# The modulation's weight transfers issued by GpSimd's queue instead of SyncE's

## The chip, the core and the metric

The kernel runs on one core of a Trainium2 chip. The metric is the time of one execution on the device, in microseconds (us), measured as the median of several runs. The core's engines are PE (TensorE, the matmuls, with its weight loads shown apart as PEld), DVE (VectorE), ACT (ScalarE), POOL (GpSimd) and SP (SyncE). Each engine works through its own row of instructions in order, and a transfer (DMA) is started by an instruction that stands in the row of one of them; what starts transfers is called that engine's queue here. A transfer's time to landing is counted from the start of the instruction that issues it.

## The reference, cut to what is touched

The whole computation is two blocks on 512 tokens of width 1024. The first block is a mixer (an mLSTM and a dilated attention, side by side) followed by a product-key layer of experts (PEER). The second block has two layers, each an attention and a convolutional feed-forward, both modulated by vectors that come from a condition `c`. What the change touches is the making of these vectors:

```
silu_c = jax.nn.silu(c)
silu_cc = jax.nn.silu(c_ctx)
for i in range(DEPTH_2):                      # 2 layers
    mod = silu_c @ w_mod[i] + b_mod[i]        # w_mod[i] is 1024 x 6144, float32
    mod_c = silu_cc @ w_mod[i] + b_mod[i]
    sh1, sc1, gt1, sh2, sc2, gt2 = jnp.split(mod[:, None, :], 6, axis=-1)
    ...
    h = modulate(rmsnorm(x, g_attn[i]), sh1, sc1)
```

Nothing of `mod` depends on `x`, so the kernel makes the vectors of both layers while the first block runs.

## The kernel before

Activations lie transposed, 8 tiles of 128 features by 512 tokens. Most products are made of three matmuls of split operands: a float32 weight tile is loaded (`wload`, lines 186 to 189, tile `wraw`, three buffers), ACT makes its high part `wh` (line 183), DVE the low part `wl` (line 184), and PE runs `hh,wh`, `hl,wh` and `hh,wl` (lines 206 to 208 in `proj`). All transfers of `wload` are issued by SP, in its row's order.

The modulation is the generator `modulation(mp_, pmod, ly)` (line 379 on). For a layer `ly` it goes over 3 groups, 8 steps `k` and 2 halves: 48 transfers of 512 KB each, 96 in all, and each loads a tile `mraw` that is used by four small matmuls (line 392, eight PE rows in the trace: 128x32 weights, 256 columns) and then not again. `mraw` has two buffers, so a transfer is issued as soon as PE has finished the four matmuls of the tile two before it: at any time at most two of these tiles are ahead of PE. At a group's end the sums are copied to `mrow` by ACT (line 397) and transposed by PE (line 347).

`fill(n)` advances the generator by n steps of `k` (two tiles each). It is called between other work: layer 0's 48 tiles are used during the mixer (from the program's start to about 308 us of the trace), layer 1's during the query stage of the experts (about 365 to 555 us). There, for each of 8 heads and each of 2 halves, the kernel issues a transfer of `keys` on POOL (line 854), makes a projection of a `w_query` tile, calls `fill(1 + half)`, runs some early products of experts (line 814), and makes the scores `sc` (line 863), whose best 16 DVE picks (`top16`, lines 841 to 848). After both halves POOL adds candidates (`cand`, line 871), which DVE searches again.

A scheduler of the framework puts the instructions of every engine into order: it gives the work priorities, keeps its own estimate of when each operand is ready, and writes one fixed row per engine. Nothing is reordered on the chip. At the start, POOL's row holds the loads of constants (`cload`, line 161: `ccols`, `cols`, `bmod` and so on), the table of the attention's bias (`t5oh`, `t5ln`, `relb`, lines 445 to 447) and `t5d` (line 453); SP's row holds the eight tiles of `XT`, then `mraw` and the weights. `norm_split` at the start runs with high priority: squares on ACT (line 258), their sum `nsum` on DVE, `ncol` (line 263) and `nbc` (line 271) on PE, then `nh`, `hh` and `hl`, from which the gates' product `gps` (lines 206 to 208) is made.

Of the kernel before, what the change touches and what calls it, by code (L numbers as in the profile page):

```python
# [107 lines left out]
def body(ctx: ExitStack, tc: tile.TileContext, a: dict, out: bass.AP, dbg=None, stop=None):  # L108
# [8 lines left out]
    ve, se, pe, gp, sy = nc.vector, nc.scalar, nc.tensor, nc.gpsimd, nc.sync  # L117
# [41 lines left out]
    def cload(pl, name, shape, dt=F32):  # L159
        t = pl.tile(shape, dt, name=name)  # L160
        gp.dma_start(t, a[name])
        return t
# [183 lines left out]
    def transpose(ps, src):  # L346
        pe.transpose(ps, src, ident[:src.shape[0], :src.shape[0]])  # L347
# [32 lines left out]
    def modulation(mp_, pmod, ly):  # L380

        bm = cload(mp_, "bmod", [128, 2, 48])
        for g in range(3):
            ps = pmod.tile([128, 512], F32, name="mod")
            for k in range(KT):
                for hf in range(2):

                    raw = mp_.tile([128, 4, 256], F32, name="mraw", bufs=2)
                    sy.dma_start(raw, a["w_mod"][ly, g, k, hf])
                    for c in range(4):  # L390
                        o = 32 * c
                        pe.matmul(ps[o:o + 32, hf * 256:hf * 256 + 256], sc[:, k], raw[:, c],  # L392
                                  start=k == 0 and hf == 0, stop=k == KT - 1 and hf == 1, tile_position=(0, o))
                if k < KT - 1:
                    yield
            rows = mp_.tile([128, 512], F32, name="mrow")
            se.activation(rows, ps, AF.Copy)
            tp = pmod.tile([128, 4, 128], F32, name="mod")
            for b_ in range(4):
                transpose(tp[:, b_], rows[:, b_ * 128:(b_ + 1) * 128])  # L400
            tv = tp.rearrange("p b (c r) -> p c b r", c=4)
            s = slice(g * 16, g * 16 + 16)
            bv = bm[:, ly, s].rearrange("p (c b) -> p c b", c=4)
            for dst, r_ in ((modx, 0), (modc, 1)):
                ve.tensor_tensor(dst[:, ly, s].rearrange("p (c b) -> p c b", c=4), tv[:, :, :, r_], bv, OP.add)
            yield
        for m_, gm in ((modx, gmx), (modc, gmc)):
            for i in range(2):
                ve.scalar_tensor_tensor(gm[:, ly, i * 8:i * 8 + 8], m_[:, ly, i * 24 + 8:i * 24 + 16], 1.0,
                                        c2[:, ly, i * 8:i * 8 + 8], OP.add, OP.mult)  # L410
# [13 lines left out]
    with ExitStack() as mx:  # L424
        mp_ = pool(mx, "mod")
        pmod = pool(mx, "pmod", 1, space=PS)
        ho = pool(mx, "mho")
        ml_ = mx.enter_context(ExitStack())
        ph["mod"] = modulation(mp_, pmod, 0)
        hp = pool(ml_, "mh")  # L430
        wk = pool(ml_, "mwork", 2)
# [337 lines left out]
    with ExitStack() as ex:  # L769
# [10 lines left out]
        hf = XT  # L780
# [53 lines left out]
        with ExitStack() as gx:  # L834
            mp_ = pool(gx, "mod")
            kp_ = pool(gx, "topk")
            ph["mod"] = modulation(mp_, pmod, 1)
            v16 = kp_.tile([128, 4, 16, 16], F32, name="v16")
            i16 = kp_.tile([128, 4, 16, 16], U32, name="i16")
# [959 lines left out]
```

## Time and profile before

| | |
|---|---|
| median of 3 runs | 3386.69 us (3386.09 to 3388.05) |
| the profiled execution | 3394.01 us, of which the trace's span is 3391.3 us |
| PE busy | 3279.6 us (97% of the span) |
| DVE busy | 2353.6 us (69%) |
| ACT busy | 1237.5 us (36%) |
| POOL busy | 681.4 us (20%) |

The profiled execution is 7.3 us above the median of the runs, and 2.7 us of it lie around the span. Busy shares are taken over a program with very different stages: the first 36 us, for one, hold the first loads and little for PE to do, and some stages of the mixer and of the experts leave PE idle, while most of the rest is PE end to end. PE's clock is shown as granted, 1.00 for 2.4 GHz and 0.50 for 1.2 GHz.

### The profile page before, as it was taken

To read this page: it belongs to the slowest core of one execution; us is meant where nothing else is said; L and a number is where in the kernel's file an instruction comes from. 1 tells how busy PE (TensorE), PEld (TensorE's weight loads), DVE (VectorE), ACT (ScalarE), POOL (GpSimd) and SP (SyncE) were. 2 spreads that over 40 slices of the span, in tenths; PEclk is the share of its full clock that TensorE was granted. 3 is DMA by queue.
4 is the path that set the end of the run, shared out by engine and by line. 5 is a ranking of instruction groups with operands and counts; after the bars stand their busy time and mean duration, and the time that the engine had idled before them with its cause. 6 is when DMAs were issued, how large, how long until landed. Compare 5 with 4: busy or idle time off the path is not lost.

```text
span 3391.3 us, 49822 instructions
## 1 busy us (share of the span) xinstructions
PE 3279.6 (97%) x19091; PEld 2761.6 (81%) x19091; DVE 2353.6 (69%) x4718; ACT 1237.5 (36%) x2137; POOL 681.4 (20%) x695
## 2 busy tenths in 40 slices
PE   8899999899999999999999999999999998989999
PEld 5565666678999999999989887898888887878887
DVE  6345678876777767777765557677776778758776
ACT  5135211564333333333354546321221246633221
POOL 0000011564444444444411222000000001100000
PEclk9899999999999999999999999999999999999999
DMA  5544564459888889888832222222112110023231
GB/s 172 185 126 158 177 208 149 152 207 330 300 313 309 305 289 331 303 313 315 311 112 76 69 73 66 67 87 63 63 63 66 59 43 28 14 76 118 94 99 56
DMA packets 151990, 538.07 MB, mean 159 GB/s; under 512 B 17988, under 2 KB 23332, under 8 KB 150216
## 3 DMA queue, kind: packets, MB, share of 16 engines
q1 hardware_dynamic: 97920, 326.76, 28.9%
q0 software_dynamic: 52800, 205.51, 17.0%
q8 instruction: 150, 2.46, 0.3%
q10 hardware_dynamic: 1032, 2.62, 0.2%
q14 instruction: 88, 0.72, 0.1%
HBM read 497.24 MB, written 40.13 MB: 158 GB/s over the span
## 4 chain that ended last, share of the span: by engine, by line
PE 86%; DVE 7%; DMA 2%; issue 2%; ACT 2%; POOL 1%; SPq 0%; DVEq 0%; POOLq 0%; ACTq 0%
PE pv L1100 15%; PE acc L206 11%; PE acc L208 11%; PE acc L207 11%; PE acc L232 9%; PE pd L200 3%; PE pd L199 3%; PE pd L201 3%; PE acc L814 3%; PE pt L347 2%; DMA mraw<-in_w_mod_dram 2%; PE mod L392 2%; PE gps L978 1%; PE on L1401 1%; DVE eb L960 1%
## 5 line engine op out<-in xcount | busy, mean ns | idle before, releaser
L206 PE MATMUL acc<-hh,wh 128*128 128x512 f32 (+1 forms) x1728 | 636.4, 369 | 6.3 <-DVE cg L1206 2.3
L207 PE MATMUL acc<-hl,wh 128*128 128x512 f32 (+1 forms) x1728 | 632.4, 366 | 0.0
L208 PE MATMUL acc<-hh,wl 128*128 128x512 f32 (+1 forms) x1728 | 632.1, 366 | 0.0
L206 PEld LDWEIGHTS acc<-hh,wh 128*128 128x128 f32 x1728 | 325.4, 188 | 52.6 <-issue 7.9
L207 PEld LDWEIGHTS acc<-hl,wh 128*128 128x128 f32 x1728 | 325.4, 188 | 38.8 <-issue 0.9
L208 PEld LDWEIGHTS acc<-hh,wl 128*128 128x128 f32 x1728 | 325.0, 188 | 38.6 <-issue 2.2
L183 ACT ACTIVATE wh<-wraw 128x1024 fp32r<-128x1024 f32 (+1 forms) x189 | 199.2, 1055 | 401.2 <-PE acc L207 174.1
L1100 PE MATMUL pv<-vh,al 128*128 128x512 f32 x768 | 301.0, 392 | 0.0
L1100 PE MATMUL pv<-vl,ah 128*128 128x512 f32 x768 | 300.7, 392 | 0.0
L1100 PE MATMUL pv<-vh,ah 128*128 128x512 f32 x768 | 298.8, 389 | 0.0
L184 DVE TENSOR_TENSOR wl<-wraw,wh 128x1024 fp32r<-128x1024 f32 (+1 forms) x189 | 230.8, 1222 | 97.6 <-ACT wh L183 94.0
L1016 POOL DMA_INDIRECT rows<-in_expert_v_dram,sidx x128 | 193.9, 1515 | 231.9 <-DVE tok L1031 198.3
L1016 POOL DMA_INDIRECT rows<-in_expert_u_rows_dram,sidx x128 | 176.8, 1382 | 238.1 <-DVE rows L1021 214.4
L232 PE MATMUL acc<-wh,hh 128*128 128x256 f32 (+1 forms) x624 | 195.9, 315 | 3.9 <-ACT hh L183 2.3
L232 PE MATMUL acc<-wh,hl 128*128 128x256 f32 (+1 forms) x624 | 193.6, 310 | 0.0
L232 PE MATMUL acc<-wl,hh 128*128 128x256 f32 (+1 forms) x624 | 193.3, 310 | 0.0
L1074 DVE TENSOR_TENSOR al<-ge,ah 128x384 fp32r<-128x384 f32 x128 | 71.5, 559 | 163.2 <-ACT ah L1072 162.6
L1072 ACT ACTIVATE ah<-ge 128x384 fp32r<-128x384 f32 x128 | 67.3, 526 | 317.4 <-PE pv L1100 284.4
L1100 PEld LDWEIGHTS pv<-vh,al 128*128 128x128 f32 x768 | 144.1, 188 | 30.2
L1031 DVE SCALAR_TENSOR_TENSOR tok<-rows,spre,tok 128x1024 f32<-128x1024 f32 x127 | 162.6, 1280 | 7.3 <-DMA rows<-in_expert_v_dram,sidx 6.6
L1100 PEld LDWEIGHTS pv<-vl,ah 128*128 128x128 f32 x768 | 144.2, 188 | 28.1
L1100 PEld LDWEIGHTS pv<-vh,ah 128*128 128x128 f32 x768 | 144.4, 188 | 27.7
(459 smaller groups left out, 7355.2 us busy)
## 6 DMA issues: line engine op xcount, KB each, us to landing
wraw<-in_expert_u_dram SPq DMA_DIRECT2D x128, 512.0 KB, 6.2
vraw<-in_expert_v_dram SPq DMA_DIRECT2D x127, 512.0 KB, 4.8
mraw<-in_w_mod_dram SPq DMA_DIRECT2D x96, 512.0 KB, 4.3
wraw<-in_ffn_up_dram SPq DMA_DIRECT2D x88, 512.0 KB, 3.6
gt<-gdr POOLq DMA_DIRECT2D x31, 768.0 KB, 9.4
wraw<-in_ffn_down_dram SPq DMA_DIRECT2D x44, 512.0 KB, 4.1
gdr<-gst POOLq DMA_DIRECT2D x6, 2048.0 KB, 7.4
gdr<-rows POOLq DMA_DIRECT2D x6, 2048.0 KB, 7.7
```

Source lines behind the costliest of these rows:

```text
L183: se.activation(hi, src, AF.Copy)
L184: ve.tensor_tensor(lo, src, hi.bitcast(F32), OP.subtract)
L199: pe.matmul(ps, wh[i], xh[i], start=i == 0, stop=False)
L200: pe.matmul(ps, wh[i], xl[i], start=False, stop=False)
L201: pe.matmul(ps, wl[i], xh[i], start=False, stop=i == n - 1)
L206: pe.matmul(ps, wh[:, k], hh[:, k], start=k == 0, stop=False)
L207: pe.matmul(ps, wh[:, k], hl[:, k], start=False, stop=False)
L208: pe.matmul(ps, wl[:, k], hh[:, k], start=False, stop=k == KT - 1)
L232: pe.matmul(ps[:, i], x[:, k, s], y, start=k == 0 and i == 0 and x is hh and y is wh, stop=k == KT - 1 and i == nt - 1 and y is wl)
L1016: gp.indirect_dma_start(r, None, src, bass.IndirectOffsetOnAxis(ap=sidx[:, k:k + 1], axis=0))
L1031: pin(ve.scalar_tensor_tensor(o, r, spre[:, k:k + 1], o, OP.mult, OP.add))
L1100: pe.matmul(sums[t][hf], x[:, s], y[:, d], start=e == 0 and y is vh and x is ah, stop=e == NE - 1 and x is al)
```

## The change

One line of `modulation`: the transfer of `mraw` is issued by `gp` (POOL) and no longer by `sy` (SP).

```diff
                     raw = mp_.tile([128, 4, 256], F32, name="mraw", bufs=2)
-                    sy.dma_start(raw, a["w_mod"][ly, g, k, hf])
+                    gp.dma_start(raw, a["w_mod"][ly, g, k, hf])
                     for c in range(4):
```

Sizes, buffers, matmuls and bytes are the same. SP's row loses 96 instructions, POOL's gains them, and because the scheduler's estimates change with the queue, other rows change as well. Three places:

POOL's row at the start of the program, up to the write of the bias table (line 161 loads constants, lines 445 to 447 and 453 are the bias table, line 389 is `mraw`). Before:

```order
L161 DMA bmod<-in_bmod_dram 128x96
L445 DMA t5oh<-in_t5oh_dram 32x640
L446 DMA t5ln<-in_t5ln_dram 8x640
L447 DMA relb<-in_rel_bias_dram 32x8
L161 DMA gbias<-in_gbias_dram 36x1
L161 DMA sel_273<-in_sel_dram 4x512
L161 DMA col_275<-in_col_dram 128x16
L161 DMA cmaskT<-in_cmaskT_dram 128x128
L161 DMA wqk_m<-in_wqk_m_dram 128x1024
L453 DMA t5d<-t5ln 8x640
```

After:

```order
L389 DMA mraw<-in_w_mod_dram 128x1024 x2
L445 DMA t5oh<-in_t5oh_dram 32x640
L446 DMA t5ln<-in_t5ln_dram 8x640
L389 DMA mraw<-in_w_mod_dram 128x1024 x2
L447 DMA relb<-in_rel_bias_dram 32x8
L161 DMA gbias<-in_gbias_dram 36x1
L389 DMA mraw<-in_w_mod_dram 128x1024 x2
L161 DMA sel_273<-in_sel_dram 4x512
L161 DMA col_275<-in_col_dram 128x16
L161 DMA cmaskT<-in_cmaskT_dram 128x128
L161 DMA wqk_m<-in_wqk_m_dram 128x1024
L453 DMA t5d<-t5ln 8x640
```

The transfers of `mraw` now stand between the loads of constants, and from the third on each waits in this row for PE.

PE's row at the start (line 392 is the modulation, lines 263 and 271 the norm, line 451 the bias table, lines 206 to 208 the gates `gps` and the first projection `acc`). Before:

```order
L392 MATMUL mod<-mraw,silc 32x256
L263 MATMUL ncol<-ones,nsum 128x1 x4
L392 MATMUL mod<-mraw,silc 32x256 x7
L271 MATMUL nbc<-ident,ny 128x128 x4
L451 MATMUL t_263<-t5oh,relb 8x320
L392 MATMUL mod<-mraw,silc 32x256 x4
L451 MATMUL t_266<-t5oh,relb 8x320
L392 MATMUL mod<-mraw,silc 32x256 x4
L206 MATMUL acc<-hh,wh 128x512
L207 MATMUL acc<-hl,wh 128x512
L392 MATMUL mod<-mraw,silc 32x256 x8
L206 MATMUL gps<-hh,wh 36x512
```

After:

```order
L263 MATMUL ncol<-ones,nsum 128x1 x4
L271 MATMUL nbc<-ident,ny 128x128 x4
L392 MATMUL mod<-mraw,silc 32x256 x16
L451 MATMUL t_263<-t5oh,relb 8x320
L451 MATMUL t_266<-t5oh,relb 8x320
L392 MATMUL mod<-mraw,silc 32x256 x4
L206 MATMUL gps<-hh,wh 36x512
L207 MATMUL gps<-hl,wh 36x512
L392 MATMUL mod<-mraw,silc 32x256 x4
L208 MATMUL gps<-hh,wl 36x512
```

The matmuls of the first four tiles have moved behind the norm's `ncol` and `nbc`, and two matmuls of the first projection from before `gps` to behind it.

PE's row in the query stage, around one unit of a head (line 814 are early products, line 863 the scores, lines 206 to 208 the projection of the next unit). Before:

```order
L392 MATMUL mod<-mraw,silc 32x256 x8
L814 MATMUL acc<-XT,wraw 128x384 x4
L863 MATMUL sc<-keys,pq 128x128 x4
L206 MATMUL acc<-hh,wh 128x512
L207 MATMUL acc<-hl,wh 128x512
L208 MATMUL acc<-hh,wl 128x512
L392 MATMUL mod<-mraw,silc 32x256 x4
```

After:

```order
L392 MATMUL mod<-mraw,silc 32x256 x8
L814 MATMUL acc<-XT,wraw 128x384 x4
L863 MATMUL sc<-keys,pq 128x128 x3
L392 MATMUL mod<-mraw,silc 32x256 x4
L863 MATMUL sc<-keys,pq 128x128
L206 MATMUL acc<-hh,wh 128x512
L207 MATMUL acc<-hl,wh 128x512
L208 MATMUL acc<-hh,wl 128x512
L392 MATMUL mod<-mraw,silc 32x256 x4
```

The first single tile after the scores is used four matmuls earlier, ahead of the last score; this comes in seven of the eight heads. Between 88 and 365 us of the trace PE's row is the same but for two exchanges of neighbours.

## Rows read from the trace of the kernel before

**Rows 1.** The page: busy time of PE, and the chain that ended last.

```profile
PE 3279.6 (97%) x19091; PEld 2761.6 (81%) x19091; DVE 2353.6 (69%) x4718; ACT 1237.5 (36%) x2137; POOL 681.4 (20%) x695
...
PE 86%; DVE 7%; DMA 2%; issue 2%; ACT 2%; POOL 1%; SPq 0%; DVEq 0%; POOLq 0%; ACTq 0%
```

**Rows 2.** The tile mraw: its issues, PE's waits for it (us, times), landing.

```profile
L389 SPq DMA_DIRECT2D mraw<-in_w_mod_dram x96: 327/328/659, 4.5 to 548.9; - x96
...
  PE mod L392: 22.0, 18
...
DMA to landing us min/median/max: 3.3/4.3/8.7
```

**Rows 3.** Windows: start:end, us, busy PE, PEld, DVE, ACT, POOL, PEclk, DMA share, GB/s.

```profile
0.00:36.00 36.00, 21.68 (x98) 9.66 (x99) 21.20 (x41) 15.25 (x25) 8.28 (x20) 1.00 0.75 255
...
149.00:182.00 33.00, 18.46 (x115) 9.18 (x114) 4.54 (x15) 2.29 (x7) 0.00 (x0) 0.67 0.54 186
...
264.00:303.00 39.00, 32.51 (x260) 17.34 (x259) 24.19 (x88) 20.95 (x61) 4.30 (x8) 0.83 0.68 229
...
365.00:377.00 12.00, 7.65 (x52) 4.85 (x51) 4.78 (x10) 2.79 (x6) 0.00 (x0) 0.72 0.80 240
377.00:555.00 178.00, 175.81 (x1004) 117.88 (x1005) 130.99 (x745) 33.05 (x47) 22.77 (x72) 1.00 0.58 195
```

**Rows 4.** Issues: start us, us, engine, line; then groups; then KB, median landing.

```profile
164.53 1.08 PE L392 MATMUL mod<-mraw,silc 128*32 128x256 f32 x8 [3.15 <-DMA mraw<-in_w_mod_dram]
...
165.67 0.33 SPq L389 DMA_DIRECT2D mraw<-in_w_mod_dram  x1
...
388.47 1.14 PE L863 MATMUL sc<-keys,pq 128*128 128x128 f32 x8
...
389.91 0.54 POOL L854 DMA_DIRECT2D keys<-in_keys_dram  x1 [26.27 <-PE sc L863]
...
L854 POOL DMA_DIRECT2D keys<-in_keys_dram x16 | 8.7, 541 | 150.4 <-PE sc L863 121.6 <-PE ya L742 28.8
...
L184 DVE TENSOR_TENSOR wl<-wraw,wh 128x1024 fp32r<-128x1024 f32 (+1 forms) x189 | 230.8, 1222 | 97.6 <-ACT wh L183 94.0
...
rank<-in_rank_dram POOLq DMA_DIRECT2D x1, 512.0 KB, 7.8
na_mask<-in_na_mask_dram POOLq DMA_DIRECT2D x1, 512.0 KB, 3.4
```

**Rows 5.** Timeline of ACT and PE at the start [idle before <-releaser].

```profile
10.34 1.15 ACT L258 ACTIVATE nsq<-XT 128x512 f32<-128x512 f32 x2
...
11.56 1.03 PE L392 MATMUL mod<-mraw,silc 128*32 128x256 f32 x2 [11.56 <-ACT nsq L258]
...
16.20 2.08 PE L271 MATMUL nbc<-ident,ny 128*128 128x128 f32 x8
...
27.67 1.08 PE L392 MATMUL mod<-mraw,silc 128*32 128x256 f32 x8 [0.58 <-DMA mraw<-in_w_mod_dram]
```

**Rows 6.** The chain of waits of 145 to 180 us, pieces in time.

```profile
143.70 8.72 DMA mraw<-in_w_mod_dram
...
161.44 4.29 DMA mraw<-in_w_mod_dram
```

**Rows 7.** PE's timeline, two waits for mraw in the mixer and behind it.

```profile
268.81 0.64 PE L392 MATMUL mod<-mraw,silc 128*32 128x256 f32 x8 [1.64 <-DMA mraw<-in_w_mod_dram]
...
372.28 1.06 PE L392 MATMUL mod<-mraw,silc 128*32 128x256 f32 x2 [1.75 <-DMA mraw<-in_w_mod_dram]
```

**Rows 8.** PE's timeline in the query stage, two units of heads.

```profile
441.56 0.64 PE L392 MATMUL mod<-mraw,silc 128*32 128x256 f32 x8 [1.41 <-DMA mraw<-in_w_mod_dram]
...
458.52 1.07 PE L392 MATMUL mod<-mraw,silc 128*32 128x256 f32 x16
...
462.21 1.05 PE L863 MATMUL sc<-keys,pq 128*128 128x128 f32 x8
...
463.90 0.64 PE L392 MATMUL mod<-mraw,silc 128*32 128x256 f32 x8
```

## The prediction, made before the changed kernel ran

> **What bounds the kernel now.** I read the page first: PE is busy for 97% of the span, and 86% of the chain that ended last is PE's own work [rows 1]. A reader should see from this that almost any wait of PE, anywhere, is added to the time, and that nothing else is: POOL is idle for four fifths of the span, so that its own issue time is not a price by itself. Then the tile that is moved: its 96 issues run from 4.5 to 548.9 us, a transfer lands 3.3 to 8.7 us after its issue, and PE stood idle for 22.0 us in 18 waits because a tile had not come [rows 2]. So the transfers of the modulation are on the path in places, and the windows say where: PE is short of work in 0 to 36, in 149 to 182 (18.46 us busy of 33.00), in 264 to 303 and in 365 to 377; in the query stage, 377 to 555, it is busy for 175.81 of 178.00 us, with DVE at 130.99 [rows 3]. The stages between show no such wait. After 555 us no tile is used any more, and what is late there is late to the end. In each stage a tile has two buffers, so the loop "PE ends, queue issues, data lands, PE starts" is a chain of its own wherever PE has nothing else to run.
>
> **What one issue costs.** On SP an issue starts 0.06 us behind the matmul that frees the buffer (164.53 + 1.08 = 165.61, issue at 165.67) and takes 0.33 us. On POOL a freed buffer of `keys` shows 389.91 against 388.47 + 1.14 = 389.61, that is 0.30 us, and 0.54 us for the issue [rows 4]. A transfer that waits for PE thus starts 0.24 us later, and the second of a pair that is freed together 0.21 us later again. For the landing itself the nearest row is a transfer of the same 512 KB from POOL's queue: `na_mask` lands in 3.4 us [rows 4], no longer than the shortest of `mraw` on SP, 3.3 [rows 2]. I take the same landing for both queues, and 0.3 us as the price of a link of the chain; with a second transfer on the way it may be longer (`rank`, the same size on POOL's queue beside transfers on SP's, took 7.8 us [rows 4]) or shorter, because the tile no longer lies behind a weight tile on SP's queue. The 96 x 0.54 = 52 us of issue time on POOL find an engine with 22.77 us of work in 178 in the query stage [rows 3], and are priced at nothing beyond these 0.3 us.
>
> The Trainium skill ("DMA: Bandwidth & Descriptors", section "Latency and other measured facts") gives a first byte after about 0.6 us for transfers issued by SyncE and about 1 us for those of GpSimd. By its difference a link would cost about 0.4 us where the rows give 0.3, and the sum below would be about 1 us higher.
>
> **The start, 0 to 36 us: +3.5 (1 to 6.5).** Before, SP issues the eight tiles of `XT` and then the first two of `mraw`, one queue, so `XT` has the way to itself. Now POOL issues these two at about the same moment on a queue of its own, and they share the transfer engines with the last `XT` tiles. The norm hangs on these: ACT's last two squares start at 10.34 [rows 5]. 1 MB more ahead of them, at the 255 GB/s of this window [rows 3], is 4 us if all of it came first and nothing if none did; part of `XT` is in by then, and I take +1.5 (0 to +2.5). Second, PE's row has changed: before, the matmuls of the first two tiles stand ahead of `nbc` and run in the time in which the norm's square root is made, from 11.56 to 16.20 [rows 5]; now `ncol` and `nbc` come first, and the four tiles behind them. Tiles 2 to 5 come two by two through two buffers, and tile 5 has to be there for `gps`, whose third matmul stands behind it. Before, tile 5 starts at 27.67 [rows 5]. Its chain is now: `nbc` ends some 2 us after its start, tiles 0 and 1 take 2.1, then two landings of 4 to 4.5 us with matmuls of 1.1 and 0.3 us of issue each. With `nbc` at 16 this comes to 16 + 2 + 2 + 2 x (4.3 + 0.3 + 1.1) = 31.4 for the end of tile 5, where it was 28.7; two matmuls of `gps` are done by then, which gives back 0.9. I take +2 (1 to 4). Constants that now stand behind waits on POOL (`relb`, `gbias`) land before PE wants them, since their users stand behind the same tiles. What covers the two projection matmuls that moved is `gps` itself.
>
> **36 to 149 us: 0.** PE's work covers all these transfers, with more room than 0.3 us at each.
>
> **149 to 182 us: +1.3 (0.5 to 2.5).** Here PE has nothing but the end of layer 0's second group. The chain is links such as 161.44, a landing of 4.29 us and eight matmuls [rows 6]. Four or five links follow one another in it, each 0.3 us later: +1.3. The slow one of 8.72 us is a transfer beside two weight tiles [rows 6]; what it does on another queue is the lower end.
>
> **264 to 303: +0.6 (0 to 1.5). 365 to 377: +0.5 (-0.5 to +2).** Two pairs of waits of the kind at 268.81, 1.64 us, and one wait of 1.75 at 372.28 [rows 7], each with one link that starts 0.3 us later; the second now competes with `rank` on its own queue.
>
> **The query stage, 377 to 555: +5.2 (-0.8 to +11.5).** A unit: two tiles are used at 458.52, the first buffer is free 0.64 us later, at 459.16; then come the early products, the scores at 462.21, and the third tile at 463.90 [rows 8]. That is 4.74 us for issue and landing, against a median of 4.3 [rows 2]: it just fits. Now the third tile stands behind three of four scores, that is at about 462.8 to 463.0, and its issue starts at 459.46. With landings of 3.4 to 4.8 it is there at 462.9 to 464.3, so PE waits for 0 to 1.3 us; I take 0.75, near the median landing. The fourth tile, issued 0.5 us behind, is wanted 2 us later and lands some 1.3 later: 0 to 0.65, I take 0.3. Seven heads have this order: 7 x 1.05 = 7.4. The waits that are there already, at most 178.00 - 175.81 = 2.2 us [rows 3], the largest of them 1.41 at 441.56 [rows 8], lie at these same tiles and are part of it, not on top: +5.2. Bounds: 7 x 0.2 - 2.2 = -0.8 and 7 x 1.95 - 2.2 = 11.5. POOL's row has `cand` between some of these transfers, and `cand` waits for DVE; the transfers next to it are the ones for tiles five to eight of a head, which are wanted later than before.
>
> **The sum.** 3.5 + 0 + 1.3 + 0.6 + 0.5 + 5.2 = 11.1 us. The profiled execution of 3394.0 would become 3405.1; carried to the median of the runs, 7.3 us lower, 3397.8. I write 3398. The lower bounds of all terms come to 0, the upper to 24, so this case covers 3387 to 3411.
>
> **The rivals.** (a) The query stage stays covered, within 0.2%. `mraw` no longer stands behind weight tiles on SP's queue, so landings come near 3.4 us and the third tile is just in time; then that term is at its lower end and the sum 11.1 - 6.0 = 5.1, about 3392. For it: the shortest landings [rows 2, 4]. Against it: both queues feed the same transfers, and the weight tile of the next unit is on the way in the same microseconds.
> (b) Faster. If a queue of its own shortens every landing that was above the median, the long waits go: 1.64, 1.75, 1.41 [rows 7, 8], an estimated 2.5 of the 4.4 us by which 8.72 exceeds the median [rows 2, 6], and their like, some 10 of the 22.0 us [rows 2]. With the start at its lower bound this gives -9, about 3378. It decides from the point where a tile beside a weight tile lands within 4 us. Against it: `rank`, on the other queue beside SP's transfers, took 7.8 us [rows 4].
> (c) POOL's issue is held up by DVE. If it could start only at the end of a running DVE instruction, a link would cost up to the 1.2 us of a `wl` [rows 4] in place of 0.3; over 25 links (the 18 waits of [rows 2] and seven new ones) this is up to 23 us more, 3398 + 12 to 23, or 3410 to 3421. Against it: 16 issues of `keys` in the stage where DVE is busy for 74% took 0.54 us each, no longer than at any other place [rows 3, 4].
>
> The Trainium skill speaks for this rival: "SBUF — State Buffer", section "SBUF: two separate sides", says that a transfer issued by GpSimd has its descriptors written by GpSimd's cores, and that these are locked out while VectorE runs certain instructions on both of its ports, so that such a transfer should go to ScalarE's or SyncE's queue. The trace does not show it: the `keys` issues took 0.54 us; whether the landing suffers is not seen in these rows.
>
> **How the numbers follow.** Chances: the forecast 0.60, (a) 0.25, (b) 0.09, (c) 0.06. A measurement of this kernel can tell about 0.2% from no change, 6.8 us, so "same" is 3379.9 to 3393.5. Faster is (b), 0.09. Same is (a) and the lower tail of the forecast, 0.29. Slower is the rest of the forecast and (c), 0.62. The range of 3384 to 3410 leaves out most of (b), most of (c) and a little of the forecast's upper tail, under 0.2 together.
>
> **What would show it.** In the changed kernel's trace: `mraw` issues on POOL's queue about 0.3 us behind the freeing matmul, 0.54 us long, landing in 3.4 to 4.5; the end of `gps` about 3.5 us later than before; the window from 149 to 182 longer by 1.3; in seven heads a wait of PE for `mraw` behind the third score, about 1 us in sum, and the stage from 377 to 555 about 5 us longer; equal time behind it. Wrong would be: landings on the new queue that differ from SP's by more than a microsecond either way, an issue that starts long after its release ((c)), or waits at 268, 372 and 441 us that have gone ((b)).

## The result and the profile after

The changed kernel took 3410.71 us, the median of 6 runs (3404.27 to 3419.11), against 3388.4 us for 6 runs of the kernel before (3386.09 to 3392.81). The ratio is 1.0065, with a 95% interval of 1.0055 to 1.0076: about 22 us slower, 19 to 26. The sum had said 11 and the range ended at 3410. The direction was right, every large term was too small, and one mechanism was not in the sum at all.

The profiled execution took 3409.26 us, 15 us more than the profiled one of before, and its span is 3407.5 us. From its page, the engines' busy times and the shares of the chain (columns as in [rows 1]):

```profile
PE 3278.8 (96%) x19091; PEld 2762.0 (81%) x19091; DVE 2354.2 (69%) x4718; ACT 1238.2 (36%) x2137; POOL 731.3 (21%) x791
...
PE 79%; issue 8%; DVE 6%; DMA 4%; ACT 1%; POOL 1%; POOLq 0%; DVEq 0%; ACTq 0%
```

And the view of the tile `mraw` (columns as in [rows 2]):

```profile
L389 POOL DMA_DIRECT2D mraw<-in_w_mod_dram x96: 527/528/583, 4.5 to 567.4; - x96
...
  PE mod L392: 35.2, 24
...
DMA to landing us min/median/max: 3.6/4.6/8.3
```

PE's busy time is the same to within 0.8 us (3278.8 for 3279.6), so over the whole execution the loss is idle time of PE: the span less the busy time is 128.7 us, and was 111.7. PE's waits for a tile of `mraw` went from 22.0 us in 18 waits to 35.2 in 24. The landing is 0.3 us longer in the median (4.6 for 4.3) and in the minimum (3.6 for 3.3), so the assumption of equal landings fell. The issues stood where they were expected: 0.53 us long, some 0.33 us behind the matmul that frees the buffer.

Where the 16 us of span went is read by laying points of the two traces beside each other, in PE's row:

| point in the program | before, us | after, us | later by |
|---|---|---|---|
| start of `ncol`, the norm's sum | 12.55 | 12.66 | 0.1 |
| bias product `abps` (line 517), in the first projection | 51.18 | 57.75 | 6.6 |
| 7th tile of `mraw` used | 88.44 | 98.36 | 9.9 |
| end of the second group of tiles | 177.47 | 187.31 | 9.8 |
| 5th tile of layer 1, start of the query stage | 391.63 | 403.38 | 11.8 |
| last pair of tiles used | 552.14 | 570.92 | 18.8 |
| end of the span | 3391.3 | 3407.5 | 16.2 |

Two stretches carry it: the first 98 us (9.9) and the query stage (7.0). The row of the second group hides two things that cancel: by the use of its 9th tile the delay had fallen to 8.1 us (168.43 for 160.31), and the chain of tiles behind it brought 1.7 of that back.

One pair of traces does not give the size of the start. The kernel before and the experiments with its rows at the start use the 7th tile at 88.4 to 92.8 us in seven traces, and the trace of the kernel before is the earliest; with the new rows it is at 96.2 to 100.3 in three (the changed kernel, e2 and e4 below). The means lie 7.6 us apart, close to what e2's time gives (7.5).

**The start** reads like this in the chain of waits of the changed kernel (start us, us, what):

```profile
20.18 5.07 DMA mraw<-in_w_mod_dram
...
26.37 2.24 PE t L451 x4
28.63 7.11 DMA wraw<-in_w_u_dram
...
36.86 1.24 DVE wl L184
38.11 4.21 DMA wraw<-in_w_u_dram
...
57.75 0.61 PE abps L517 x2
```

The tile of `mraw` in its first line is the one that the prediction followed. But the chain does not go on to the gates `gps`, as I had it: it goes over the bias table's matmuls to the loads of the first projection's weights, `w_u`. Those wait for buffers of `wraw`, which the gates' weight and the two tiles of the bias table hold. Before, the first `w_u` was issued at 16.75 us, because DVE made the low half of the gates' weight at 15.59 and so gave its buffer back:

```profile
15.59 0.46 DVE L184 TENSOR_TENSOR wl<-wraw,wh 128x288 fp32r<-128x288 f32 x1
16.75 0.37 SPq L188 DMA_DIRECT2D wraw<-in_w_u_dram  x1
35.34 0.74 DVE L473 TENSOR_SCALAR li<-gps,gbias 4x512 f32<-4x512 f32 x1 [2.27 <-PE gps L208]
51.18 0.40 PE L517 MATMUL abps<-abd,ones 4*128 4x32 f32 x2 [1.14 <-DVE abd L515]
```

Now that instruction stands behind the whole norm in DVE's row, at 29.58, and the first `w_u` is issued at 28.63, when PE has done with the bias table. What this does to DVE, DVE's timeline in the changed kernel shows (start us, us, what, and in brackets the idle time ahead and what ended it):

```profile
29.58 0.43 DVE L184 TENSOR_TENSOR wl<-wraw,wh 128x288 fp32r<-128x288 f32 x1
36.86 1.22 DVE L184 TENSOR_TENSOR wl<-wraw,wh 128x1024 fp32r<-128x1024 f32 x1 [6.84 <-ACT wh L183]
39.62 1.23 DVE L184 TENSOR_TENSOR wl<-wraw,wh 128x1024 fp32r<-128x1024 f32 x1 [1.54 <-ACT wh L183]
40.76 0.73 DVE L473 TENSOR_SCALAR li<-gps,gbias 4x512 f32<-4x512 f32 x1
```

And PE's timeline at the bias product behind it:

```profile
57.75 0.61 PE L517 MATMUL abps<-abd,ones 4*128 4x32 f32 x2 [4.82 <-DVE abd L515]
```

The gates' first step, `li`, is ready to run near 38 us, when `gps` ends, but stands in the row behind two splits of weights that come late. It starts at 40.76; before it was 35.34. From there a chain of small DVE steps runs to `abd`, for which PE has to wait 4.82 us (1.14 before). Here the wait has an echo, in the windows (columns as in [rows 3]):

```profile
44.00:51.00 7.00, 7.00 (x33) 5.79 (x32) 5.42 (x11) 6.60 (x8) 0.00 (x0) 1.00 0.55 154
51.00:58.00 7.00, 2.18 (x11) 1.53 (x9) 7.00 (x21) 3.35 (x5) 0.00 (x0) 0.99 0.19 38
58.00:65.00 7.00, 7.00 (x21) 5.56 (x22) 6.83 (x12) 6.25 (x9) 0.00 (x0) 0.53 0.36 112
```

PE is busy for 2.18 of 7 us, and in the 7 us behind that its granted clock is 0.53 in the mean, almost all of it at the lower of the two levels (0.50), with PE busy throughout. From 6.6 us at `abps` the delay grows to 9.9 us in this stretch.

**The query stage**: PE's timeline at two heads.

```profile
474.12 0.83 PE L863 MATMUL sc<-keys,pq 128*128 128x128 f32 x6
476.11 0.64 PE L392 MATMUL mod<-mraw,silc 128*32 128x256 f32 x8 [1.17 <-DMA mraw<-in_w_mod_dram]
...
497.21 0.83 PE L863 MATMUL sc<-keys,pq 128*128 128x128 f32 x6
501.06 0.67 PE L392 MATMUL mod<-mraw,silc 128*32 128x256 f32 x8 [3.02 <-DMA mraw<-in_w_mod_dram]
```

This answers [rows 8]: the tile behind the third score is there some 1.2 us late, at the place that was forecast. In one head it is 3.02 us late. PE's waits for tiles there sum up to 8.7 us.

### The profile page after: what moved, and what is told of

Its sections match the earlier page's. It is cut to its first block, busy times and chain, and to the rows that moved or that the text cites. A ratio compares the mean times of both kernels' runs of the same rounds, so it can differ in the third digit from the quotient of the medians.

```text
span 3407.5 us, 49816 instructions
## 1 busy us (share of the span) xinstructions
PE 3278.8 (96%) x19091; PEld 2762.0 (81%) x19091; DVE 2354.2 (69%) x4718; ACT 1238.2 (36%) x2137; POOL 731.3 (21%) x791
## 4 chain that ended last, share of the span: by engine, by line
PE 79%; issue 8%; DVE 6%; DMA 4%; ACT 1%; POOL 1%; POOLq 0%; DVEq 0%; ACTq 0%
PE pv L1100 15%; PE acc L206 11%; PE acc L208 11%; PE acc L207 11%; PE acc L232 8%; DMA mraw<-in_w_mod_dram 3%; PE pd L200 3%; PE pd L199 3%; PE pd L201 3%; PE pt L347 2%; PE acc L814 2%; PE gps L978 1%; PE on L1401 1%; DVE eb L960 1%; PE mod L392 1%
## 5 line engine op out<-in xcount | busy, mean ns | idle before, releaser
L1100 PEld LDWEIGHTS pv<-vh,al 128*128 128x128 f32 x768 | 144.1, 188 | 30.2
```

Of the source, the lines that this page charges most:

```text
L1100: pe.matmul(sums[t][hf], x[:, s], y[:, d], start=e == 0 and y is vh and x is ah, stop=e == NE - 1 and x is al)
```

## The experiments

Two theories. **A: the rows.** The new order of rows costs, at the start by the weights that come late, in the query stage by a slot ahead of the landing; the queue itself costs only where transfers stand in a chain. **B: the queue.** Every transfer that POOL issues is late by its issue and landing, wherever it is waited for, and so is other work beside it (DVE, the weights on the way). e1, e3 and e4 have 5 runs each, the others 11 or 12; microseconds behind a ratio are the ratio's excess times 3390 us.

### Which part of the transfers costs

Each of four kernels puts only some tiles on POOL's queue; the four new lines are those of e1, e2, e3 and e4, one in each kernel:

```diff
-                    gp.dma_start(raw, a["w_mod"][ly, g, k, hf])
+                    (sy if ly == 0 and g == 0 and k < 3 else gp).dma_start(raw, a["w_mod"][ly, g, k, hf])
+                    (gp if ly == 0 and g == 0 and k < 3 else sy).dma_start(raw, a["w_mod"][ly, g, k, hf])
+                    (gp if ly == 1 else sy).dma_start(raw, a["w_mod"][ly, g, k, hf])
+                    (gp if ly == 0 else sy).dma_start(raw, a["w_mod"][ly, g, k, hf])
```

> The first six tiles of layer 0 are issued by SP, the other 90 by POOL; the rows of PE, ACT and DVE at the start are those of the kernel before. Theory A (the rows' order at the start costs some 10 us, behind it only the transfers that PE waits for cost): the window 0 to 98 us is that of the kernel before, the rest costs what the query stage showed, 6 to 9 us, so the time is about 8 us over the kernel before (3394 to 3400). Theory B (every transfer on POOL's queue costs its later issue and longer landing, wherever it is waited for): with 90 of 96 tiles still on POOL, at least 15 of the 22 us stay (3403 or more).

> Only the first six tiles of layer 0 are issued by POOL, the other 90 by SP; the start of all rows is that of the changed kernel. Theory A: 9 to 12 us over the kernel before, with the first modulation tile behind the gates (the seventh) used near 98 us and not 88. Theory B: at most 3 us over it, since only six transfers are later by about half a microsecond each.

> Layer 1's 48 tiles by POOL, layer 0's by SP. Theory A: the query stage is 5 to 8 us longer and nothing else changes, 3394 to 3397. Theory B: half of the tiles, so about half of the 22 us, 3397 to 3401, in about equal pieces per waited transfer. That DVE holds POOL's issue back would show as issues that start more than 0.35 us behind the matmul that frees the buffer.

> Layer 0's 48 tiles by POOL, layer 1's by SP. Theory A: 10 us from the start, 1 to 2 from the stretches without other work at 149 to 182 and 264 to 303 us: 11 to 14 us over the kernel before, and together with the kernel that has layer 1 on POOL it makes up the whole change. Theory B: 11 us too, but spread over the waits of the whole first 308 us, not in the first 98.

| kernel | tiles on POOL | ratio to the kernel before | us |
|---|---|---|---|
| e1 | all but the first six | 1.0050 (1.0037 to 1.0064) | +17.0 |
| e2 | the first six | 1.0022 (1.0013 to 1.0031) | +7.5 |
| e3 | layer 1 | 1.0048 (1.0034 to 1.0062) | +16.3 |
| e4 | layer 0 | 1.0041 (1.0027 to 1.0054) | +13.9 |

Six tiles of 96 cost a third of the change: this is what A says of the start (9 to 12 us) in kind, and B (at most 3) does not. In e2's trace the loads of `w_u` are late as well (the first at 29.49 us) and in the chain of waits, but they hold up the gates at another place: `li` starts as soon as `gps` ends (40.56), and a later step, `ra`, stands in ACT's row behind the split of the last `w_u` at 47.29.

But layer 1 costs 16.3 us where A had 5 to 8, and e1 came out in B's range. e3 and e4 together make 30.2, more than the 22 of the change; with intervals of 4 to 5 us to either side of each this is at the edge of what adds. The view of PE's waits in the query stage tells where e3's time went (us in total, times, the longest; first the changed kernel, then e3):

```profile
PE mod L392 <- DMA mraw<-in_w_mod_dram: 8.7, 7, 3.0
```

```profile
PE mod L392 <- DMA mraw<-in_w_mod_dram: 11.3, 7, 3.0
```

The waits are the same seven, at the same slots, but the long ones of 2 to 3 us come more often: in e3 three heads, in the changed kernel one. From the fifth tile of layer 1 to its last the stage is 6.8 us longer in the changed kernel's trace, 9.2 in e3's and 12.1 in e1's, so it varies from one execution to the next by as much as I had forecast for all of it. e3's trace does not place all of its 16.3 us: 2.7 us of its delay had arisen before layer 1's first tile was used, where its queue and its rows are those of the kernel before. The issues in e3 that PE waited for all started 0.33 us behind the freeing matmul, under the 0.35 from which DVE was to be suspected.

### Putting the rows right, with the queue left on POOL

The second four hold rows back by an edge of order between instructions of PE (no wait is added). At the start, the norm's matmuls are held behind those of the first two tiles, nearly as before; ACT and DVE then split the gates' weight early again. In the query stage, the two tiles wanted behind a head's scores are used behind nine matmuls of the next projection. The first part of the diff is in e5 and e8, the second in e6, e7 and e8; `held` is the last instruction recorded so far, which is a matmul, and e5 and e6 have their tiles on POOL as e2 and e3 have:

```diff
-        fill(3)
+        fill(1)
+        held = nc.cur_bb.bb.instructions[-1]
+        fill(2)
         hh, hl = split_tile("h"), split_tile("l")
-        norm_split(XT, T, cols[:, 0:8], hh, hl)
+        with tc.issue_after(held):
+            norm_split(XT, T, cols[:, 0:8], hh, hl)
...
-                    proj(ps, wunit(a["w_query"][u]), h)
-                    fill(1 + half)
+                    w = wunit(a["w_query"][u])
+                    proj(ps, w, h, range(3))
+                    held = nc.cur_bb.bb.instructions[-1]
+                    if hd and not half:
+                        with tc.issue_after(held):
+                            fill()
+                    proj(ps, w, h, range(3, KT))
+                    fill(2 if u == 15 else 1)
```

> As the kernel that has only the first six tiles on POOL's queue (8.2 us over the kernel before), but the norm's matmuls are held behind those of the first two tiles, which gives PE, ACT and DVE nearly their rows of before: the gates' weight is split ahead of the norm's halves, its buffer comes free early, and the first projection's weights are loaded early. Theory A (the rows make the start late): at most 3 us over the kernel before, with the first w_u load issued before 20 us and the bias product abps within 2 us of its time before. Theory B (POOL's queue makes it late, by its issue or by sharing the way with XT): 6 us or more stay.

> Layer 1's tiles on POOL, as in the kernel that was 15 us over the one before; the two tiles that are wanted right behind a head's scores are used behind nine matmuls of the next projection instead. Theory A (the slot, ahead of the landing, costs): PE's waits for mraw in the query stage fall from some 9 to 11 us to under 2, and the time comes to within 4 us of the kernel before. Theory B (each transfer on POOL's queue makes other work later, by DVE, POOL or by the weights that share the way): the waits go, but 8 us or more of the 15 stay.

> The kernel before, all tiles on SP, with the same later slots in the query stage. Both theories: 1 to 3 us faster than the kernel before, by its waits of 2.2 us there.

> The changed kernel, all tiles on POOL, with both repairs of rows: the start's and the later slots. Theory A: 2 to 7 us over the kernel before, which is what the links at 149 to 182 and 264 to 303 us cost through POOL's later issue and landing. Theory B: 15 us or more over it, near the changed kernel's 22.

| kernel | tiles on POOL, rows | ratio to the kernel before | us | without the new rows |
|---|---|---|---|---|
| e5 | first six; start's rows held | 0.9992 (0.9983 to 1.0000) | -2.7 | e2: +7.5 |
| e6 | layer 1; later slots | 1.0003 (0.9992 to 1.0014) | +1.0 | e3: +16.3 |
| e7 | none; later slots | 0.9989 (0.9978 to 0.9999) | -3.7 | 0 |
| e8 | all; both | 1.0025 (1.0015 to 1.0035) | +8.5 | the change: +22.0 |

Here A holds and B falls. With the same six tiles on POOL and other rows, the 7.5 us of the start are gone. `abps` starts at 54.21, 3.0 us later than before where 2 were expected, but the seven traces with the rows of before have it at 51.18 to 54.15. In SP's timeline of e5 the first `w_u` is issued at 17.15 us, some 0.4 us from where it was before:

```profile
17.15 0.33 SPq L188 DMA_DIRECT2D wraw<-in_w_u_dram  x1
```

And in PE's timeline of e5 the wait for `abd` is back at 1.13 us (here line 520, by the edit above it):

```profile
54.21 0.40 PE L520 MATMUL abps<-abd,ones 4*128 4x32 f32 x2 [1.13 <-DVE abd L518]
```

With layer 1 on POOL and the slots moved back, 15 of the 16 us are gone, and so are most of the waits (PE's waits in the query stage of e6):

```profile
PE mod L392 <- DMA mraw<-in_w_mod_dram: 1.6, 6, 0.6
```

48 transfers still go through POOL there, beside the same row of DVE, so what was lost was lost by PE's waiting at the slot, and not by other work that POOL's transfers made late. That DVE or the shared way lengthens landings is not ruled out: in e6 five tiles of the stage land only 6.7 to 7.4 us behind their issue, at places where PE has other work. How much of the loss SP would have had at the same slot was not run. The trace of before lets one estimate it: of the six third tiles whose landing it shows, four landed 4.6 to 6.1 us behind the freed buffer and two 3.7 to 3.8, and the slot wants them some 3.9 behind it, so PE would have waited for most of them on SP too, for 0.7 us and more. Against the fair partner, e7 with the same later slots on SP, the queue's own price in the query stage is 4.7 us by the ratios, with some 5 us of interval to either side. With both repairs, the change's 22.0 us fall to 8.5, somewhat above the 2 to 7 that A had for the middle alone.

### The middle, and the two gains together

```diff
-                    gp.dma_start(raw, a["w_mod"][ly, g, k, hf])
+                    (gp if ly == 0 and g == 1 else sy).dma_start(raw, a["w_mod"][ly, g, k, hf])
+                    (gp if ly == 0 and (g, k) >= (0, 3) else sy).dma_start(raw, a["w_mod"][ly, g, k, hf])
```

The first new line is e9's, the second e10's. e11 is e5 and e7 in one kernel.

> Only layer 0's second group, 16 tiles, on POOL's queue; every row of PE, DVE and ACT is that of the kernel before, so this is the price of the queue alone. The comparison of the first two traces gives 0.27 us later issue and 0.23 us longer landing, 0.5 us for a link of the chain, and four to five links stand one behind the other at 149 to 182 us: 2 to 3 us over the kernel before. The prediction's 0.3 us a link would give 1.3. If the queue has no price beyond the rows, 0.

> Layer 0's tiles 6 to 47 on POOL, the first six and layer 1 on SP; rows at the start and in the query stage as before. Theory A (links in the stretches without other work): 4 to 6 us over the kernel before, which closes the sum of start, middle and query stage. If the middle costs nothing and the parts do not add, under 2 us.

> The first six tiles on POOL with the start's rows held as in e5, all others on SP with the later slots of e7: the two that came out at or below the kernel before, put together. 1 to 4 us faster than the kernel before if both gains are real; no change if they were noise.

e9 came to 1.0010 (1.0000 to 1.0020), +3.4 us; e10 to 1.0014 (1.0005 to 1.0023), +4.7; e11 to 1.0002 (0.9994 to 1.0011), no change. e9 is the cleanest of all, because not one row of PE, DVE or ACT differs from the kernel before. PE's timeline of e9 in the stretch where PE has only tiles to wait for:

```profile
161.59 1.07 PE L392 MATMUL mod<-mraw,silc 128*32 128x256 f32 x16
166.62 0.64 PE L392 MATMUL mod<-mraw,silc 128*32 128x256 f32 x8 [3.97 <-DMA mraw<-in_w_mod_dram]
...
171.52 1.08 PE L392 MATMUL mod<-mraw,silc 128*32 128x256 f32 x8 [2.57 <-DMA mraw<-in_w_mod_dram]
...
179.55 1.08 PE L392 MATMUL mod<-mraw,silc 128*32 128x256 f32 x8 [1.63 <-DMA mraw<-in_w_mod_dram]
```

And the same stretch of the kernel before, whose second row is in [rows 4], with a wait of 3.15:

```profile
160.31 1.07 PE L392 MATMUL mod<-mraw,silc 128*32 128x256 f32 x16
...
169.19 1.08 PE L392 MATMUL mod<-mraw,silc 128*32 128x256 f32 x8 [2.34 <-DMA mraw<-in_w_mod_dram]
...
176.39 1.08 PE L392 MATMUL mod<-mraw,silc 128*32 128x256 f32 x8 [1.32 <-DMA mraw<-in_w_mod_dram]
```

From the first row to the last it is 17.96 us in e9 and 16.08 before: 1.9 us for a chain of three issues and landings, 0.6 us each. That agrees with what the two first traces give tile by tile, in the median: from the freed buffer to the landing 0.51 us more, 0.27 by the issue and the rest by the landing. The other traces bear it out: from the first row to the last it is 15.99 to 17.04 us in the seven with this group on SP and 17.69 to 18.40 in the six with it on POOL (17.80 in the changed kernel). The time of e9 adds a little more, but its interval begins at no change. So the links have their price, about twice the 0.3 that I used, and the whole middle costs 4.7 us (1.7 to 7.8); with the start's 7.5 and layer 1's 16.3 the parts make 28.5, where the change is 22.0 (18.6 to 25.8). The intervals of the parts, 3 to 5 us to either side, allow that, but the sum is not shown closer than this. e7 alone came out below the kernel before by more than its interval, and its gain with that of e5 did not come back in e11, so no version here is shown to beat the kernel before.

## Why the prediction was wrong, step by step

**What bounds it.** Right: PE's work stayed the same, and the loss is PE's waiting. POOL's issue time, priced at nothing by itself, shows no cost of its own: POOL's busy time rose by 50 us, and e6, with half of these issues, is 1.0 us (-2.7 to 4.7) from the kernel before.

**The price of a link.** Too small: 0.3 us, from the issue alone. The step that failed is "I take the same landing for both queues": it rested on one transfer, `na_mask`, that ran on POOL's queue with no weight tile beside it. Measured 0.5 to 0.6. The stretch 149 to 182 us came out at 1.9 us in e9 (1.3 forecast), and no farther off because a second error went the other way: three links stand one behind the other there, not four or five. For the middle, 4.7 us (1.7 to 7.8) where two terms of 1.9 were forecast, the interval leaves it open. The Trainium skill ("DMA: Bandwidth & Descriptors", section "Latency and other measured facts") has the first byte come after about 0.6 us for SyncE's transfers and about 1 us for GpSimd's, an estimated 0.4 us later by the difference. The trace agrees in direction: counted from the issue's start the landing is 0.3 us longer in the median (4.6 for 4.3). The prediction put this difference in the place of its 0.3 us, though the 0.3 held the later issue alone; the two add up.

**The start.** 3.5 us forecast (1 to 6.5), 7.5 measured in e2 (4.4 to 10.5). Of its two parts, the shared way of `XT` and `mraw` was wrong: +1.5 forecast, 0.1 in the trace (`ncol` at 12.66 for 12.55). The other, +2, had the gates' product right (it ends 2.7 us later), but that end is not what the time hangs on: in e5 it comes later still, at 39.47 us for 37.96 in the changed kernel, and the loss is gone. What failed is the step "what covers the two projection matmuls that moved is `gps` itself". I followed PE's row only. DVE's row had moved too, and with it the time at which a buffer came free, the weights that waited for this buffer, and the gates' chain that stands behind the splits of these weights, on DVE in the changed kernel, on ACT in e2. e5 shows that it is the rows, since it leaves the queue and turns the rows back; that it is DVE's row and the buffer among them is read from the traces: the loads of `w_u` are in the chain of waits with the new rows, in e5 the first of them is early again, and from `li` to `abps` it takes 14.7 us, where it took 15.8 before, 17.0 in the changed kernel and 20.2 in e2.

**The query stage.** The place, the mechanism and the seven heads were right; the size was not: +5.2 forecast (up to 11.5), 6.8 to 12.1 in three traces and 16.3 (11.5 to 21.0) by e3's time. The slot comes about 3.9 us behind the freed buffer, as I had it (3.6 to 3.8). For the landing I took 3.4 to 4.8 us over all tiles, and a wait of 0.75 near their median. Of the seven tiles that are used at this very slot, five land beside an expert's and a query's weight tile; there 4.3 to 4.7 us, and in one case 5.0, is the rule: a wait of 0.8 to 1.4. The last two heads, with one weight tile, wait 0.3 to 0.6. In one to three heads of a trace the tile is there only 5.6 to 6.8 us behind its issue, a wait of 2 to 3.5 (the traces of the changed kernel, e1 and e3), and four of these six waits were followed by a stretch at the lower clock. This is the term that was sized too small: a third tile was priced at 0.75, and the seven waits make 8.7 us in the changed kernel, 1.2 each. The fourth tile's 0.3 us a head never came: in none of the three traces does PE wait for it. So the forecast comes nearer to the changed kernel's trace (5.2 for 6.8) than its parts do, by luck. e6 shows that it is the slot, by moving it.

**The rivals.** (a), that the stage stays covered, and (b), that a queue of its own shortens the landings, fell by the landings: 4.6 us in the median for 4.3, and 8.7 us of waits in the stage. (c), that DVE holds back POOL's issue, gave the nearest time to the measured one, but not by its mechanism: the issues that PE waited for started 0.33 to 0.42 us behind their release, 0.33 in the query stage. The Trainium skill's rule for it ("SBUF — State Buffer", section "SBUF: two separate sides") is not borne out by these issues. Whether DVE has a part in the longer landings was not tried: e6 has the same transfers beside the same row of DVE and costs 1.0 us, but PE does not wait for its late tiles.

**The range.** It ended at 3410, since the chances left out the upper bounds of the terms; the median is 0.7 us above that. The bounds themselves, 24 us together, held the sum, but not in each term by itself: the start's ended at 6.5 where e2 has 7.5, the query stage's at 11.5 where e3 has 16.3.

## What to carry to other kernels

When a change moves rows, follow every engine's row up to the next thing that is shared, here a pool of three buffers: the engine that gives the buffer back late may be one that the change doesn't name. Price a landing by the tiles that land at the place in question, beside the transfers that are under way there, not by one transfer elsewhere. And a scheduler's slot that lies just ahead of a landing can cost more than the queue that was changed: moving two uses a head by nine matmuls took back 15 of 16 us (with some 6 us of interval to either side).

## What was not expected of the hardware

The clock can charge for a wait a second time. In the changed kernel at 51 to 58 us PE was idle for 4.8 of 7 us, and in the window behind it the granted clock was 0.53 with PE busy throughout, and the delay grew from 6.6 to 9.9 us. In its query stage the wait of 3.02 us was followed by the same (granted clock 0.63 from 502 to 506 us), the waits of 1.0 to 1.4 us were not. But the length of the wait does not tell whether it comes: at `abps`, PE waits for 1.10 to 1.14 us in nine traces, and in five of them (e1, e5, e8, e9, e11) the granted clock falls to the lower level within 2 us (0.60 from 55 to 59 us in e5), in four (the kernel before, e3, e6, e7) it does not.

Two things stay open. Why some tiles at the same slot, with the same neighbours, land after 6.5 us and others after 4.5 was not tried apart. The next query weight's transfer is no sign of it: in long and in short landings alike it is issued about 3 us behind the tile, before the tile has landed. The expert's weight may be one: in the traces of the changed kernel, e1 and e3, it was issued 0.65 to 0.69 us ahead of the tile in all six long cases, and in two of the nine others, the other seven having it from 0.31 us ahead to 0.11 behind. And in two traces (the changed kernel and e8) one issue on POOL started 3.0 us behind its release with nothing before it that the profile shows; its tile was not wanted until later, so it cost nothing.
